# Moving the making of an attention-bias table from behind the first stage of a transformer layer into the middle of it

## The chip, the cores and the metric

One core of a Trainium2 chip. The kernel is one program on that core: TensorE (PE), VectorE (DVE), ScalarE (ACT), GpSimd (POOL), the DMA queue of SyncE (SP), and 16 DMA engines. The metric is device time in microseconds (us); lower is better. Times inside the kernel are microseconds from the start of the profiled span.

## The reference

One layer with sliding-window attention, then a gated embedding, over 512 tokens of width 2048 in float32. Cut to what matters:

```python
hn = rmsnorm(x, norm_g)
q, k, v, gate = split(hn @ w_in)            # 32 query heads, 4 key/value heads, 64 wide
scores = einsum(q, k) * 64**-0.5 + bias     # blocks of 128 queries, 256 keys
bias   = rel_bias[t5_bucket(distance)]      # 32 buckets x 32 heads
scores = where(0 <= distance < 128, scores, -inf)
out = softmax(scores, with one sink per head) @ v
x = x + (out * silu(gate)) @ w_out
x = x + (p @ ple_proj) * sigmoid(rmsnorm(x, ple_norm) @ ple_gate)
return rmsnorm(x, final_g)
```

The bias depends only on the distance between query and key, so per head it is a vector of 128 values. The kernel keeps one vector of 384 floats per head, filled with -3e38 where the distance is outside the window. This is the **table**. It is written to DRAM once and read back from there with an overlapping access pattern, so that each row of a bias tile is a shifted piece of it.

## The kernel before

Every product is made in three matmuls of a high and a low part (`fp32r`): a high part is a cast on ACT, a low part a subtraction on DVE. Weights arrive as raw tiles by DMA and are split in this way before PE can use them.

**First stage.** A loop over `k = 0..15` (the 16 row blocks of the weights) loads a block of the transposed input (`xr`, line 190) and a block of weights (`w`, line 195) on the SP queue, splits both, and adds up two blocks of queries (`qps`), the keys (`ktps`) and the values (`vps`) in PSUM. In the turns 3 to 6 it also loads the four token blocks `xn0` to `xn3` (line 236) and squares them on ACT (line 237). In turn 9 the inverse root mean square `rstd1` is made; POOL writes it to DRAM (`rdram`, line 241) and reads it back spread over all partitions (`rb`, line 242). `rb` scales the queries (line 257) and keys (line 280) as they leave PSUM.

**The table**, lines 318 to 331, follows the stage in the program: POOL loads `rel` (line 320), fills the vector with the mask (line 321), waits for the load, makes 17 small copies (lines 324 and 329) and writes the table `tdram` to DRAM (line 331). It works in the tile `misc`, a quarter of the pool `whole`, which has four buffers. `xn0` to `xn3`, `values`, `misc`, `diffs` and the gate tiles take turns in them.

**The stretch after it.** PE goes on with the remaining query blocks. `Weights` holds the raw tiles `wraw` (loaded on line 101), the high parts `whi` (line 107, ACT) and the low parts `wlo` (line 113, DVE), three buffers each. One raw tile serves eight k-steps of three matmuls. PE runs four times eight and then six more k-steps before the first attention scores.

**Weight sums.** Later products use sums of weight blocks, made in DRAM: SP copies a block (line 672) and POOL adds another with an accumulating DMA (line 674). `sum_weights(n)` issues the n-th of these steps. The calls stand in this order:

```python
    for n in range(SUM_FIRST):        # 8: four copies on SP, the first add on POOL
        sum_weights(n)
    load_bias(0)                      # SP, line 378: reads tdram into bias0
    ...                               # then W.split() with the loads of wraw, and more sums
```

The order of PE and of SP is the order in which the program is written, in the whole kernel. From the first sums on, this holds for all engines (`during`). In the first stage and up to the table, ACT, DVE and POOL are put in order by a planner, which works with estimated times; instructions of both kinds can mix. In the program as laid out, the planner has POOL do `rdram`, `rb`, four adds of line 674, and only then lines 320 to 331.

`load_bias(0)` on line 378 waits for the table in DRAM. It has a second wait: the pool `attn` takes the storage that the pool `start` of the first stage gave back, and `bias0` lies in the bytes of `w0s15`, the split weights of turn 15. So it also waits for the last `vps` matmul of that turn (line 228) and its last subtraction (line 208). SP is one queue in order: what stands behind line 378 waits with it, first of all the next three loads of `wraw`.

Of the kernel before, what the change touches and what calls it, by code (L numbers as in the profile page):

```python
# [11 lines left out]
F32 = mybir.dt.float32  # L12
# [8 lines left out]
P = 128  # L21
KC = D // P
NB = S // P
HEADS = 32
# [9 lines left out]
BUCKETS = 32  # L34
MAX_DIST = 128
WINDOW = 128
PLE = 256
EPS = 1e-6
MASKED = -3.0e38
TOEP = 384  # L40
# [4 lines left out]
def bucket_of(dist):  # L45
    exact = BUCKETS // 2
    d = np.maximum(dist, 1).astype(np.float32)
    large = exact + (
        np.log(d / exact) / np.log(MAX_DIST / exact) * (BUCKETS - exact)
    ).astype(np.int32)  # L50
    large = np.minimum(large, BUCKETS - 1)
    return np.where(dist < exact, dist, large).astype(np.int32)
# [3 lines left out]
def trunk_kernel(ctx: ExitStack, tc: tile.TileContext, a: dict):  # L56
    nc = tc.nc
# [22 lines left out]
    def quarter(name):  # L80
        return whole.tile([P, 4, S], F32, tag="quarter", name=name)
# [39 lines left out]
    def mm3(ps, sh, sl, mh, ml, first, last, more=False):  # L121


        nc.tensor.matmul(ps, sh, mh, start=first, stop=False, skip_group_check=more)  # L124
        nc.tensor.matmul(ps, sh, ml, start=False, stop=False, skip_group_check=more)  # L125
        nc.tensor.matmul(ps, sl, mh, start=False, stop=last, skip_group_check=more)  # L126
# [28 lines left out]
    def run(gen):  # L155
        for _ in gen:
            pass

    def rsqrt_mean(out, ssq, n, nm):

        w = out.shape[-1]
        ms = const.tile([P, w], F32, name=f"ms_{nm}")
        rt = const.tile([P, w], F32, name=f"rt_{nm}")
        y = const.tile([P, w], F32, name=f"y_{nm}")
        t = const.tile([P, w], F32, name=f"t_{nm}")
        nc.vector.tensor_scalar(ms, ssq, 1.0 / n, EPS, op0=ALU.mult, op1=ALU.add)
        nc.scalar.activation(rt, ms, AF.Sqrt)
        yield
        nc.vector.reciprocal(y, rt)
        nc.vector.tensor_mul(t, y, y)  # L170
        nc.vector.tensor_mul(t, t, ms)
        nc.vector.tensor_scalar(t, t, -0.5, 1.5, op0=ALU.mult, op1=ALU.add)
        nc.vector.tensor_mul(out, y, t)

    kinds, upto = [], {"q": 2, "g": 0}
    for kind in "qq" + "qqqqggg" * (KVH - 1) + "ggggggg":
        kinds.append((kind, upto[kind]))
# [6 lines left out]
    for k in range(KC):  # L186
        both = start_pool.tile([P, 2, 768], F32R, tag="w0s", name=f"w0s{k}")
        wh, wl = both[:, 0], both[:, 1]
        xg = start_pool.tile([P, S + 1], F32, tag="xr", name=f"xr{k}")
        nc.sync.dma_start(xg, a["xT"][k * P : (k + 1) * P, :])  # L190
        xr, g1 = xg[:, :S], xg[:, S:]
        w0 = w0s[0] if k == 0 else start_pool.tile([P, 768], F32, tag="w0", name=f"w0_{k}")
        cuts = [slice(512, 768), slice(0, 512)] if k == 0 else [slice(0, 768)]
        for c in cuts[-1:]:
            nc.sync.dma_start(w0[:, c], a["w_first"][k][:, c])
        room = acts if k < KC // 2 else more
        h = room.tile([P, S], F32R, tag="ah", name=f"xh{k}")
        l = room.tile([P, S], F32R, tag="al", name=f"xl{k}")
        nc.scalar.mul(h, xr, g1)
        if k == 0:  # L200
            nc.vector.tensor_copy(wh[:, cuts[0]], w0[:, cuts[0]])
            nc.vector.tensor_sub(wl[:, cuts[0]], w0[:, cuts[0]], wh[:, cuts[0]].bitcast(F32))
        nc.vector.scalar_tensor_tensor(
            out=l, in0=xr, scalar=g1, in1=h.bitcast(F32), op0=ALU.mult, op1=ALU.subtract
        )
        for c in cuts[-1:]:
            nc.scalar.copy(wh[:, c], w0[:, c])
            nc.vector.tensor_sub(wl[:, c], w0[:, c], wh[:, c].bitcast(F32))
        xh.append(h)
        xl.append(l)  # L210
        f, e = k == 0, k == KC - 1
        qc = [slice(512 + t * P, 512 + (t + 1) * P) for t in range(2)]
        if f:
            for n, (sw, mx) in enumerate(((wh, h), (wl, h), (wh, l))):
                for t in range(2):
                    nc.tensor.matmul(q_ps[t], sw[:, qc[t]], mx, start=n == 0, stop=False)
        else:
            for t in range(2):
                mm3(q_ps[t], wh[:, qc[t]], wl[:, qc[t]], h, l, f, e)
        for t in range(2):  # L220
            c = slice(t * P, (t + 1) * P)
            mm3(kt_ps[t], wh[:, c], wl[:, c], h, l, f, e)
        for t in range(NB):
            c = slice(t * P, (t + 1) * P)

            for part in "hl" if f else "lh":
                if part == "h":
                    nc.tensor.matmul(v_ps[t], h[:, c], both[:, :, 256:512], start=f, stop=e, skip_group_check=True)  # L228
                else:
                    nc.tensor.matmul(  # L230
                        v_ps[t][:, :256], l[:, c], wh[:, 256:512], start=False, stop=False, skip_group_check=True
                    )
        if 3 <= k < 3 + NB:
            t = k - 3
            xn = quarter(f"xn{t}").rearrange("p k t -> p (k t)")
            nc.sync.dma_start(xn, a["x"][t * P : (t + 1) * P, :])
            nc.scalar.activation(xn, xn, AF.Square, accum_out=ssq1[:, t : t + 1])
        if k == 9:
            run(rsqrt_mean(rstd1, ssq1, D, "r1"))
            rdram = tc.dram_tile([NB, P], F32, name="rdram")  # L240
            nc.gpsimd.dma_start(rdram.rearrange("t p -> p t"), rstd1)
            nc.gpsimd.dma_start(rb, rdram.rearrange("t p -> (t p)").partition_broadcast(P))
        if k == 10:
            for h in range(GROUP):
                nc.sync.dma_start(sinkb[QB * h : QB * h + QB], a["sinks"][h].partition_broadcast(QB))
            nc.sync.dma_start(pn, a["ple_norm"])
# [67 lines left out]
        )  # L314
    split(V[0], values[0])


    misc = quarter("misc")
    relb, tvec = misc[:HEADS, 1, :BUCKETS], misc[:HEADS, 2, :TOEP]
    nc.gpsimd.dma_start(relb, a["rel"])  # L320
    nc.gpsimd.memset(tvec, MASKED)
    exact = BUCKETS // 2
    bk = bucket_of(np.arange(WINDOW))
    nc.gpsimd.tensor_copy(tvec[:, P - 1 : P - 1 + exact], relb[:, :exact])
    for b in range(exact, BUCKETS):
        d = np.nonzero(bk == b)[0]
        if len(d):
            lo, n = P - 1 + int(d.min()), len(d)
            nc.gpsimd.tensor_copy(tvec[:, lo : lo + n], relb[:, b : b + 1].to_broadcast([HEADS, n]))
    tdram = tc.dram_tile([HEADS, TOEP], F32, name="tdram")  # L330
    nc.gpsimd.dma_start(tdram, tvec)

    pre.close()
    banks_s.close()
# [1210 lines left out]
    n = done[3]  # L1545
# [87 lines left out]
```

## Time and profile before

| | |
|---|---|
| median of 3 runs | 792.78 us (791.22 to 794.69) |
| the profiled execution | 791.03 us |
| its span | 789.3 us |
| PE busy | 778.5 us (99%) |
| DVE, ACT, POOL busy | 623.7, 506.5, 180.4 us |
| granted TensorE clock, mean | 0.997 |

The span is the time between the first and the last instruction of the profiled execution; 1.7 us of its time lie around it. Busy PE means that a matmul was in progress. The page cuts the span in 40 slices: PE shows 9 tenths or more in all but the last. The DMA engines show 6 tenths or more in all but the last two slices.

### The profile page before, as it was taken

What the parts mean: (1) busy time and instruction counts of PE and PEld (TensorE: products, weight loads), DVE (VectorE), ACT (ScalarE), POOL (GpSimd) and SP (SyncE); (2) the same over time, 40 slices, a digit from 0 to 9 for tenths busy, and PEclk for the clock granted to TensorE, in tenths of its full rate; (3) what the DMA queues carried; (4) which work ended last, traced back from release to release, by engine and by line L of the source; (5) the groups of instructions that cost most, each with busy time, mean ns of one, the idle gap of its engine ahead of it and who ended that gap; (6) DMA issues with size and microseconds to landing.
All of it is one profiled execution on the core that took longest, in us unless ns stands there. A gap on an engine that the chain in (4) does not pass through costs nothing.

```text
span 789.3 us, 11284 instructions
## 1 busy us (share of the span) xinstructions
PE 778.5 (99%) x3726; PEld 650.0 (82%) x3726; DVE 623.7 (79%) x1056; ACT 506.5 (64%) x1024; POOL 180.4 (23%) x394
## 2 busy tenths in 40 slices
PE   9999999999999999999999999999999999999995
PEld 8888788888888888888888888888888888888885
DVE  4446468887977788787886798999798988999686
ACT  5632366667666666565665655767788857967465
POOL 0002423544344414444143300200000021101000
PEclk9999999999999999999999999999999999999998
DMA  8797799999999999989997497998778999967833
GB/s 332 282 251 189 259 280 331 297 290 300 305 312 245 309 268 275 278 212 246 294 245 208 136 352 288 245 367 281 249 272 248 365 238 251 255 227 215 256 117 118
DMA packets 50634, 206.99 MB, mean 262 GB/s; under 512 B 7264, under 2 KB 8416, under 8 KB 44208
## 3 DMA queue, kind: packets, MB, share of 16 engines
q1 hardware_dynamic: 40240, 156.15, 54.7%
q0 software_dynamic: 9904, 49.61, 32.8%
q8 instruction: 29, 0.48, 0.2%
q10 hardware_dynamic: 432, 0.52, 0.2%
q14 instruction: 29, 0.24, 0.1%
HBM read 199.38 MB, written 78.69 MB: 352 GB/s over the span
## 4 chain that ended last, share of the span: by engine, by line
PE 92%; DMA 3%; DVE 2%; ACT 1%; issue 1%; SPq 0%; POOL 0%; ACTq 0%; DVEq 0%; POOLq 0%
PE gps L124 7%; PE gps L125 7%; PE gps L126 7%; PE qps L124 6%; PE qps L125 5%; PE qps L126 5%; PE g L125 5%; PE o L124 5%; PE g L124 5%; PE g L126 5%; PE o L125 5%; PE o L126 5%; DMA wraw<-in_w_q 2%; PE vps L228 2%; PE s L400 2%; PE o L522 2%
## 5 line engine op out<-in xcount | busy, mean ns | idle before, releaser
L124 PE MATMUL gps<-xh,whi 128*128 128x512 f32 x256 | 100.5, 393 | 0.0
L125 PE MATMUL gps<-xl,whi 128*128 128x512 f32 x256 | 100.1, 391 | 0.0
L126 PE MATMUL gps<-xh,wlo 128*128 128x512 f32 x256 | 99.9, 390 | 0.0
L113 DVE TENSOR_TENSOR wlo<-wraw,whi 128x1024 fp32r<-128x1024 f32 x60 | 74.6, 1246 | 30.5 <-ACT whi L107 17.2
L502 POOL TENSOR_SCALAR_AFFINE_SELECT own<-r 64x256 fp32r<-64x256 f32 x96 | 60.1, 626 | 162.2 <-DVE r L491 82.7
L126 PE MATMUL qps<-xh,wlo 128*128 128x512 f32 x224 | 87.5, 391 | 0.5 <-DVE wlo L113 0.5
L124 PE MATMUL qps<-xh,whi 128*128 128x512 f32 x224 | 87.7, 391 | 0.0
L125 PE MATMUL qps<-xl,whi 128*128 128x512 f32 x224 | 87.5, 391 | 0.0
L460 ACT ACTIVATE t<-t,sm 128x129 f32<-128x129 f32 x128 | 50.7, 397 | 51.7 <-DVE sm L451 48.8
L107 ACT CAST whi<-wraw 128x1024 fp32r<-128x1024 f32 x60 | 62.2, 1038 | 20.9 <-DMA wraw<-in_w_q 20.9
L710 DVE TENSOR_TENSOR blo<-braw,bhi 128x1024 fp32r<-128x1024 f32 x43 | 52.7, 1229 | 14.9 <-ACT bhi L709 14.9
L709 ACT CAST bhi<-braw 128x1024 fp32r<-128x1024 f32 x43 | 45.0, 1050 | 28.9 <-DMA braw<-in_ple_gate 9.5
L710 DVE TENSOR_TENSOR blo<-ring,bhi 128x1024 fp32r<-128x1024 f32 x48 | 58.3, 1223 | 4.7 <-ACT bhi L709 4.3
L709 ACT CAST bhi<-ring 128x1024 fp32r<-128x1024 f32 x48 | 50.2, 1049 | 17.9 <-PE o L126 14.1
L124 PE MATMUL g<-bhi,fhg 128*128 128x512 f32 x148 | 58.0, 392 | 0.0
L125 PE MATMUL g<-blo,fhg 128*128 128x512 f32 x148 | 57.8, 391 | 0.0
L126 PE MATMUL g<-bhi,flg 128*128 128x512 f32 x148 | 57.7, 390 | 0.0
L126 PEld LDWEIGHTS gps<-xh,wlo 128*128 128x128 f32 x256 | 48.1, 188 | 10.5
L124 PEld LDWEIGHTS gps<-xh,whi 128*128 128x128 f32 x256 | 48.1, 188 | 9.1
L483 ACT CAST r<-pt 128x256 fp32r<-128x256 f32 x64 | 23.8, 371 | 49.5 <-PE pt L478 49.3
L125 PEld LDWEIGHTS gps<-xl,whi 128*128 128x128 f32 x256 | 48.1, 188 | 8.6
L126 PEld LDWEIGHTS qps<-xh,wlo 128*128 128x128 f32 x224 | 42.1, 188 | 10.0 <-DVE wlo L113 1.0
(303 smaller groups left out, 2034.4 us busy)
## 6 DMA issues: line engine op xcount, KB each, us to landing
w_out<-in_w_out POOLq DMA_DIRECT2D x32, 512.0 KB, 9.2
wraw<-in_w_gate_in SPq DMA_DIRECT2D x32, 512.0 KB, 7.7
ring<-w_out SPq DMA_DIRECT2D x32, 512.0 KB, 4.7
wraw<-in_w_q SPq DMA_DIRECT2D x28, 512.0 KB, 9.3
braw<-in_ple_gate SPq DMA_DIRECT2D x22, 512.0 KB, 5.2
ring<-in_w_out SPq DMA_DIRECT2D x18, 512.0 KB, 5.5
ple_gate<-in_ple_gate SPq DMA_DIRECT2D x16, 512.0 KB, 10.0
ple_gate<-in_ple_gate POOLq DMA_DIRECT2D x16, 512.0 KB, 7.9
```

The costliest lines, as they stand in the source:

```text
L107: nc.scalar.copy(hi, self.raw[i])
L113: nc.vector.tensor_sub(lo, raw, hi.bitcast(F32))
L124: nc.tensor.matmul(ps, sh, mh, start=first, stop=False, skip_group_check=more)
L125: nc.tensor.matmul(ps, sh, ml, start=False, stop=False, skip_group_check=more)
L126: nc.tensor.matmul(ps, sl, mh, start=False, stop=last, skip_group_check=more)
L228: nc.tensor.matmul(v_ps[t], h[:, c], both[:, :, 256:512], start=f, stop=e, skip_group_check=True)
L400: nc.tensor.matmul(s_ps[:, u, : 2 * n], st, key[:, :, first : first + n], start=True, stop=True)
L460: nc.scalar.activation(su, su, AF.Exp, bias=sm[:, u : u + 1], accum_out=sm[:, 2 + u : 3 + u])
L483: nc.scalar.copy(r[:, 0], PT[i])
L502: nc.gpsimd.affine_select(out=cols(own[places[g % 2 ^ low]]), in_=cols(r[here, low].bitcast(F32)), pattern=[[sign * QB, 2], [0, GROUP], [s ...
L709: nc.scalar.copy(hi, raw)
L710: nc.vector.tensor_sub(lo, raw, hi.bitcast(F32))
```

## The change

The lines 318 to 331 become a function `bias_table()`, which is called in turn 8 of the first stage, ahead of turn 9 with `rdram` and `rb`. The instructions are the same. `misc` is now asked for ahead of `values`, right after `xn3`. `load_bias(0)` stays where it is, and the order on PE and SP is the same.

```diff
+    def bias_table():
+
+        misc = quarter("misc")
+        relb, tvec = misc[:HEADS, 1, :BUCKETS], misc[:HEADS, 2, :TOEP]
+        nc.gpsimd.dma_start(relb, a["rel"])
+        nc.gpsimd.memset(tvec, MASKED)
+        exact = BUCKETS // 2
+        bk = bucket_of(np.arange(WINDOW))
+        nc.gpsimd.tensor_copy(tvec[:, P - 1 : P - 1 + exact], relb[:, :exact])
+        for b in range(exact, BUCKETS):
+            d = np.nonzero(bk == b)[0]
+            if len(d):
+                lo, n = P - 1 + int(d.min()), len(d)
+                nc.gpsimd.tensor_copy(tvec[:, lo : lo + n], relb[:, b : b + 1].to_broadcast([HEADS, n]))
+        tdram = tc.dram_tile([HEADS, TOEP], F32, name="tdram")
+        nc.gpsimd.dma_start(tdram, tvec)
+        return tdram
...
+        if k == 8:
+            tdram = bias_table()
         if k == 9:
             run(rsqrt_mean(rstd1, ssq1, D, "r1"))
             rdram = tc.dram_tile([NB, P], F32, name="rdram")
...
     split(V[0], values[0])
 
-
-    misc = quarter("misc")
-    relb, tvec = misc[:HEADS, 1, :BUCKETS], misc[:HEADS, 2, :TOEP]
-    nc.gpsimd.dma_start(relb, a["rel"])
...
-    tdram = tc.dram_tile([HEADS, TOEP], F32, name="tdram")
-    nc.gpsimd.dma_start(tdram, tvec)
```

More of the change, by code (lines that the diff above doesn't have):

```diff
@@ L315, in trunk_kernel @@
     split(V[0], values[0])
-    misc = quarter("misc")
-    relb, tvec = misc[:HEADS, 1, :BUCKETS], misc[:HEADS, 2, :TOEP]
[L320 to L329, printed above, removed]
-    tdram = tc.dram_tile([HEADS, TOEP], F32, name="tdram")
-    nc.gpsimd.dma_start(tdram, tvec)
     pre.close()
```

## The prediction, made before the changed kernel ran

> **What bounds the kernel now.** I read the page first, then what PE waited for, then the SP and POOL queues around the moved lines, then the timelines of ACT, DVE and PE where these end.
>
> The page, parts 1 and 4:
>
> ```profile
> span 789.3 us, 11284 instructions
> PE 778.5 (99%) x3726; PEld 650.0 (82%) x3726; DVE 623.7 (79%) x1056; ACT 506.5 (64%) x1024; POOL 180.4 (23%) x394
> ```
>
> PE is idle for 789.3 - 778.5 = 10.8 us in the whole span. Nothing that leaves the matmuls alone can bring more than that. Most of it is out of reach, as the waits of PE show (us in total, times, longest):
>
> ```profile
> PE warm_ps L145 <- PEq L1623: 0.8, 1, 0.8
> PE qps L126 <- DVE wlo L113: 0.5, 1, 0.5
> PE o L524 <- POOL own L502: 0.3, 1, 0.3
> PE qps L216 <- ACT xh L199: 0.2, 1, 0.2
> ```
>
> Two of these are the start. The rest of the 10.8 us lies in the last slice (the stretch from 750 us):
>
> ```profile
> 750.00:789.30 39.30, 30.33 (x164) 26.21 (x162) 29.91 (x66) 23.60 (x43) 0.00 (x0) 0.93 0.35 117
> ```
>
> Here PE is busy 30.33 of 39.30, so 9.0 us are the end of the work, behind the last matmul. What is left for an edit near the first stage is 0.5 + 0.3 us. That is the first result: the change can hide a lot of waiting on SP and still gain less than 1 us.
>
> What it goes after is seen on SP:
>
> ```profile
> SPq L378 <- DMA tdram<-misc: 27.2, 1, 27.2
> SPq L378 <- PE qps L126: 0.6, 1, 0.6
> ...
> 82.36 0.72 SPq L378 DMA_DIRECT2D bias<-tdram  x1
> 83.15 0.87 SPq L101 DMA_DIRECT2D wraw<-in_w_q  x2
> ```
>
> SP stands at line 378 for 27.2 us, from 55 to 82.4, for the table, and the wait for PE, long fulfilled, comes behind it. Two loads of `wraw` stand behind it. Their way to PE:
>
> ```profile
> 87.01 1.05 ACT L107 CAST whi<-wraw 128x1024 fp32r<-128x1024 f32 x1 [13.07 <-DMA wraw<-in_w_q]
> 88.09 1.23 DVE L113 TENSOR_TENSOR wlo<-wraw,whi 128x1024 fp32r<-128x1024 f32 x1 [11.91 <-PE qps L125]
> 89.37 0.51 PE L126 MATMUL qps<-xh,wlo 128*128 128x512 f32 x1 [0.53 <-DVE wlo L113]
> ```
>
> So the late table costs PE 0.53 us at 89.37. ACT was idle for 13.07 us and DVE for 11.91 us ahead of it, but PE had three split tiles in hand and used them up.
>
> And this is why the table is late (POOL, start and duration):
>
> ```profile
> 37.68 0.95 POOL L241 DMA_DIRECT2D rdram<-rstd  x1 [36.30 <-DVE rstd L173]
> 50.94 0.58 POOL L242 DMA_DIRECT2D rb<-rdram  x1 [12.31 <-DMA rdram<-rstd]
> ...
> 65.78 0.80 POOL L320 DMA_DIRECT2D misc<-in_rel  x1
> 66.31 0.71 POOL L321 MEMSET misc<- 32x384 f32 x1
> 77.89 0.19 POOL L324 COPY misc<-misc 32x16 f32<-32x16 f32 x1 [10.87 <-DMA misc<-in_rel]
> 78.02 2.08 POOL L329 COPY misc<-misc 32x3 f32<-32x3 f32 x16
> 80.39 0.54 POOL L331 DMA_DIRECT2D tdram<-misc  x1 [0.30 <-POOL misc L329]
> ```
>
> with the DMAs from issue to landing (KB, us):
>
> ```profile
> rb<-rdram POOLq DMA_DIRECT2D x1, 256.0 KB, 6.4
> ...
> tdram<-misc POOLq DMA_DIRECT2D x1, 48.0 KB, 1.8
> ...
> rdram<-rstd POOLq DMA_DIRECT2D x1, 2.0 KB, 13.0
> misc<-in_rel POOLq DMA_DIRECT2D x1, 4.0 KB, 12.0
> ```
>
> **The moved part.** The work itself is the same: two DMAs, a memset, 17 copies. Ahead of 37.68 POOL had been idle for 36.30 us, so POOL pays nothing. `misc` now follows `xn3`, so it takes the first buffer to come free, that of `xn0`, whose square ends here:
>
> ```profile
> 13.71 1.92 ACT L237 ACTIVATE xn<-xn 128x2048 f32<-128x2048 f32 x1 [1.69 <-DMA xn<-in_x]
> 15.53 0.18 ACT L237 ACTIVATION_READ_ACCUMULATOR xn<-xn 128x1 f32 x1
> ```
>
> That is 13.71 + 1.92 = 15.6, or 15.7 with the read of the sum. I let the load of `rel` start at 16. Its landing is bounded by the same kind of row: 1.8 us (the table's own write) to 13.0 us (`rdram`, the longest of the four); I take 12.0, that of the same load. It lands at 18 to 29, likeliest 28. The copies take 0.19 + 2.08 = 2.3 us, to 30.4; the write is issued by 31 and lands between 33 and 44 by the same two bounds. SP asks for it at 55. So the wait of 27.2 us is gone, with 11 us to spare in the worst of these.
>
> **What is late next on SP.** The other waits of line 378. The last matmul on `w0s15`:
>
> ```profile
> 71.58 0.40 PE L228 MATMUL vps<-w0s,xh 128*128 128x512 f32 x1
> 71.81 0.40 PE L124 MATMUL qps<-xh,whi 128*128 128x512 f32 x1
> ```
>
> It ends at 71.98, and SP goes on at about 72.1 instead of 82.36. SP gains 10.3 us, not 27. The loads of `wraw` then go out at 83.15 - 10.3 = 72.9. In the trace the first was needed by ACT 87.01 - 83.15 = 3.9 us later; with twice that as the other end it lands at 77 to 81. The cast must also wait for a free `whi` buffer, which PE gives back after one tile, 24 matmuls. From 71.81 to the wait at 89.37 - 0.53 = 88.84 PE does three tiles and two matmuls more, 74 in all, 0.23 us each; 24 take 5.5 us, so the buffer is free at 77.3. The low part is then ready 1.05 + 1.23 us after 77.3 to 81, at 79.6 to 83.3. PE needs it at 88.84. At least 5.5 us to spare: the 0.53 us is gone in full.
>
> Of the 0.26 us at 132 I count half. It hangs on another chain:
>
> ```profile
> 132.03 0.39 PE L524 MATMUL o<-own,DV 128*128 128x256 f32 x1 [0.26 <-POOL own L502]
> ...
> 102.38 2.44 SPq L363 DMA_DIRECT2D DV<-diffs  x4
> ```
>
> SP has caught up before that point: line 363 at 102.38 waits for DVE in the attention loop, not for earlier loads. So from 102 on SP runs as before, and only the DMA backlog of 85 to 102 is smaller, which may or may not move POOL by a quarter of a microsecond. Ends 0 and 0.26, middle 0.13.
>
> **Costs of the new place.** The added DMA bytes are 52 KB beside
>
> ```profile
> 16.00:24.00 8.00, 8.00 (x40) 6.70 (x40) 3.36 (x4) 5.53 (x7) 0.00 (x0) 1.00 1.03 417
> ```
>
> 417 GB/s, so 0.12 us of full DMA engines. The loads of the stage have cover for it, since SP itself waits for free buffers there:
>
> ```profile
> SPq L190 <- DVE xl L203: 12.2, 8, 2.7
> SPq L195 <- DVE w0s L208: 11.7, 8, 3.1
> ```
>
> Without that cover it would cost those 0.12 us. On POOL the table is now ahead of `rdram`. POOL is free of it at 31 at the latest that I count, `rdram` is due at 37.68, so nothing is added. If it were, the slack is:
>
> ```profile
> 68.56 1.44 DVE L257 TENSOR_TENSOR rawq<-qps,rb 128x256 f32<-128x256 f32 x4 [4.91 <-PE qps L126]
> ```
>
> `rb` lands at 50.94 + 6.4 = 57.3; its first reader starts at 68.56 and waited for PE. PE asks for the first freed bank at 71.81, two of those four reads (0.72 us) later than 71.1. So `rb` may come 13.7 us later, and `rdram` be issued as late as 51.4, before PE stops. POOL's new wait is the one for the load of `rel`, up to 29. Behind it stand `rdram`, `rb` and four adds, and DVE waits for `rb`; that is the slack just named. After the four adds POOL finds the next add instead of the table, and SP issues the copy for it 10.3 us sooner. `values` now takes the buffer of `xn1`, free long before 71.
>
> **The sum.** 0.53 + 0.13 = 0.66 us off 791.03 us of the profiled execution: 790.4. The median of the runs is 1.75 us above that execution, so the median to expect is 792.78 - 0.66 = **792.1 us**. A measurement of this kernel tells about 0.5%, 4 us, from no change; this gain is a sixth of that.
>
> **The rivals.**
>
> *More gain than the profile shows.* The profiled execution, 791.03 us, is the quickest of the four times that I have. PE paid 0.53 us because the chain of `rel`, table, `bias0` and `wraw` was just that much too late, and each further microsecond of a DMA in it costs PE one. If the other executions are slower for this reason, the median falls to 790.4, the sum for the profiled one. For it: the DMAs of POOL vary between 1.8 and 13.0 us. Against: nothing in one trace shows the others. Chance 0.12. Even this is inside 0.5%, but for a tail of 0.03.
>
> *The planner leaves the table where it was.* POOL's order in this stage is the planner's, which put the table behind four adds before. If it still does so, the time stays at 792.8. Against: that order came with `misc` having to follow `values`, which is made at 71; now it follows `xn3`. Chance 0.08.
>
> *Slower: `rb` comes late.* POOL is held in the table past 51.4, and PE stops at 71.81 for the excess. For this the load of `rel` would have to land at 48.5, 32 us after its issue and 2.5 times the longest row; or the copies be stretched. Suppose `misc` gets the last of the four buffers (that of `xn3`, free at 29.1: its square is the last of the four) and lands at 42.1, and each of the 17 copies finds DVE in an instruction of up to
>
> ```profile
> 26.24 0.96 DVE L208 TENSOR_TENSOR w0s<-w,w0s 128x768 fp32r<-128x768 f32 x1
> ...
> 28.90 0.18 ACT L237 ACTIVATION_READ_ACCUMULATOR xn<-xn 128x1 f32 x1
> ```
>
> 0.96 us: 17 x 0.96 = 16.3 us more, free at 42.1 + 2.3 + 16.3 + 0.5 = 61.2, and PE stops for 61.2 - 51.4 = 9.8 us. That gives 792.8 + 9.8 = 802.6 at the far end, 797 to 798 halfway. In the trace of before the copies ran while DVE was idle (its row at 88.09 shows 11.91 us), so this price isn't seen there. The Trainium skill, "SBUF — State Buffer", section "Who interferes with whom", says that a DVE instruction with two SBUF inputs and a GpSimd instruction that reads SBUF shut each other out for a whole instruction; lines 203 and 208 are of that kind. By that rule the copies would be stretched at the new place, though only with both mishaps of place and landing would it reach PE; no run here shows it yet. Against the rival: with `xn0`'s buffer the table ends at 30.4 + 16.3 = 46.7 even then, still ahead of 51.4. Chance 0.12.
>
> **How the numbers follow.** Forecast (a stall gone, nothing else) 0.68, more gain 0.12, nothing moved 0.08, slower 0.12. The three runs of before lie 1.6 us below and 1.9 us above their median, so the forecast's own range is 790.4 to 794.5. Its lower end also holds the rival with more gain. I set the range at 789.8 to 795.2, which leaves out most of the slower rival and a little at either end. Faster by over 0.5% (under 788.8): the tail of 0.03 and 0.02 of scatter, 0.05. Slower by over 0.5% (over 796.7): 0.10 of the rival's 0.12, and 0.02 of scatter, 0.12. Within: 0.83.
>
> **What would show it.** Right: POOL's load of `rel` at 16, its copies before 32, `rdram` still at 37.7; SP at line 378 near 72 with a wait for PE in place of the table; the next `wraw` near 73; no wait of PE on line 113; PE idle for about 10.1 us. Wrong: `rdram` after 51 and DVE's first read of `rb` after 71; the four adds still ahead of the table; or a wait of PE over 1 us anywhere past 72.

## The result, and the profile after

| | median | its runs | profiled execution | its span |
|---|---|---|---|---|
| before | 793.94 us | 791.22 to 795.03 (6 runs) | 791.03 us | 789.3 us |
| after | 789.09 us | 788.95 to 790.41 (6 runs) | 789.11 us | 787.4 us |

The ratio is 0.9945, 95% interval 0.9926 to 0.9964: faster by 4.85 us in the medians. Between the two profiled executions it is 1.92 us. The forecast was a gain of 0.66 us, to 792.1 us, in a range of 789.8 to 795.2; the median of before is 1.2 us higher here than in the three runs that it started from. The median of after lies just under that range. The direction and the way were right, and the size was not.

PE and the chain on the page after:

```profile
span 787.4 us, 11284 instructions
PE 777.4 (99%) x3726; PEld 649.3 (82%) x3726; DVE 621.9 (79%) x1056; ACT 506.3 (64%) x1024; POOL 182.6 (23%) x394
...
PE 98%; DMA 0%; ACT 0%; DVE 0%; issue 0%; ACTq 0%; DVEq 0%
```

and what PE waited for after (us in total, times, longest):

```profile
PE warm_ps L145 <- PEq L1628: 0.8, 1, 0.8
PE qps L234 <- ACT xh L217: 0.2, 1, 0.2
```

Two waits are left, both at the start. The chain that ended last is 98% PE. The same line of the page before had a part of DMA in it:

```profile
PE 92%; DMA 3%; DVE 2%; ACT 1%; issue 1%; SPq 0%; POOL 0%; ACTq 0%; DVEq 0%; POOLq 0%
```

POOL after (start, duration, in brackets the idle time before):

```profile
16.20 0.70 POOL L181 DMA_DIRECT2D misc<-in_rel  x1 [14.83 <-ACT xn L255]
...
21.84 0.19 POOL L185 COPY misc<-misc 32x16 f32<-32x16 f32 x1 [4.48 <-DMA misc<-in_rel]
21.97 2.84 POOL L190 COPY misc<-misc 32x3 f32<-32x3 f32 x16
25.11 0.53 POOL L192 DMA_DIRECT2D tdram<-misc  x1 [0.31 <-POOL misc L190]
37.37 0.79 POOL L261 DMA_DIRECT2D rdram<-rstd  x1 [11.73 <-DVE rstd L173]
```

The write of the table is issued at 25.11, and `rdram` follows at 37.37, where it stood at 37.68 before. SP after, its waits at `load_bias(0)` (now line 383):

```profile
SPq L383 <- DVE w0s L226: 9.5, 1, 9.5
...
SPq L383 <- PE vps L246: 7.0, 1, 7.0
```

the timeline with its issues, and the first cast and subtraction that came late before:

```profile
71.72 0.72 SPq L383 DMA_DIRECT2D bias<-tdram  x1
72.50 0.87 SPq L101 DMA_DIRECT2D wraw<-in_w_q  x2
...
81.52 1.05 ACT L107 CAST whi<-wraw 128x1024 fp32r<-128x1024 f32 x1 [7.87 <-DMA wraw<-in_w_q]
...
82.60 1.22 DVE L113 TENSOR_TENSOR wlo<-wraw,whi 128x1024 fp32r<-128x1024 f32 x1 [6.71 <-PE qps L126]
```

SP still stands there, but for the storage of `w0s15` and only to 71.72. The low part starts at 82.60, PE needs it near 88: the stall is gone.

### The profile page after: what moved, and what is told of

Its sections match the earlier page's. It is cut to its first block, busy times and chain, and to the rows that moved or that the text cites. A ratio compares the mean times of both kernels' runs of the same rounds, so it can differ in the third digit from the quotient of the medians.

```text
span 787.4 us, 11284 instructions
## 1 busy us (share of the span) xinstructions
PE 777.4 (99%) x3726; PEld 649.3 (82%) x3726; DVE 621.9 (79%) x1056; ACT 506.3 (64%) x1024; POOL 182.6 (23%) x394
## 4 chain that ended last, share of the span: by engine, by line
PE 98%; DMA 0%; ACT 0%; DVE 0%; issue 0%; ACTq 0%; DVEq 0%
PE gps L124 7%; PE gps L125 7%; PE gps L126 7%; PE qps L124 7%; PE qps L126 7%; PE qps L125 7%; PE g L125 5%; PE g L124 5%; PE o L126 5%; PE o L125 5%; PE g L126 5%; PE o L124 5%; PE s L405 2%; PE o L527 2%; PE vps L246 2%; PE pt L483 2%
## 5 line engine op out<-in xcount | busy, mean ns | idle before, releaser
L113 DVE TENSOR_TENSOR wlo<-wraw,whi 128x1024 fp32r<-128x1024 f32 x60 | 73.5, 1226 | 25.3 <-ACT whi L107 17.3
```

The lines of the kernel that those rows point to most:

```text
L113: nc.vector.tensor_sub(lo, raw, hi.bitcast(F32))
```

## The experiments

**The question** was where the other 4 us come from. Three accounts were weighed. (1) SP standing at `load_bias(0)` costs, by more than the one stall that the profile of before showed. (2) POOL, held by the table, costs: its next add, the differences of the values and the first selects come late. (3) Part of it is memory traffic or chance, and would be seen in `before` at any place. Each text on record names its own theories; theory 1 is account (1) in all of them, and theory 2 one of the other two. Medians are compared among kernels that ran on the same chip beside the same runs of before.

All runs. "SP" is when SP passes `load_bias(0)`. The DMA share and the idle time of PE are from the table by windows of each profile (PE idle is the window less PE's busy time), in us:

| kernel | median (runs) | ratio to before, 95% | SP | DMA share 72-85 / 85-100 | PE idle 85-100 / 120-145 |
|---|---|---|---|---|---|
| before (profile of the prediction) | | | 82.36 | 0.27 / 1.00 | 0.53 / 0.26 |
| again | 793.52 (12) | 1.0003, 0.9982 to 1.0023 | 83.06 | 0.30 / 1.01 | 1.13 / 1.06 |
| again2 | 792.75 (1) | | 82.71 | 0.28 / 1.01 | 1.17 / 0.51 |
| after | 789.09 (6) | 0.9945, 0.9926 to 0.9964 | 71.72 | 0.88 / 1.01 | 0 / 0 |
| times2 | 795.91 (12) | 1.0031, 1.0013 to 1.0049 | 84.55 | 0.29 / 0.91 | 2.53 / 0 |
| times3 | 798.14 (9) | 1.0060, 1.0038 to 1.0083 | 87.37 | 0.29 / 0.75 | 5.29 / 0 |
| unblock | 793.36 (12) | 1.0010, 0.9991 to 1.0030 | 91.13 | 0.96 / 0.49 | 0 / 0.39 |
| unblock4 | 791.43 (12) | 0.9964, 0.9944 to 0.9983 | 92.12 | 1.01 / 0.78 | 0 / 0 |
| after_rb | 789.63 (6) | 0.9939, 0.9919 to 0.9960 | 71.74 | 1.00 / 1.03 | 0 / 0 |
| both | 789.74 (6) | 0.9938, 0.9919 to 0.9958 | 71.61 | 1.02 / 1.02 | 0 / 0 |
| hole | 798.64 (6) | 1.0052, 1.0033 to 1.0072 | 77.74 | 0.96 / 0.91 | 0 / 0 |
| pool_busy | 790.21 (12) | 0.9953, 0.9933 to 0.9972 | 72.31 | 0.95 / 0.98 | 0 / 0 |
| pool_late | 793.64 (12) | 0.9999, 0.9975 to 1.0023 | 82.41 | 0.38 / 1.02 | 1.09 / 1.33 |
| after_times3 | 789.55 (10) | 0.9948, 0.9928 to 0.9968 | 71.31 | 0.82 / 1.01 | 0 / 0 |

The kernel before had a median of 793.11 (32 runs, 790.94 to 799.59) beside again to unblock, 794.25 (17 runs) beside unblock4 to hole, and 793.53 (29 runs, 790.40 to 798.36) beside the last three and again2; `after` has the runs of the first table beside it.

**again, again2: the kernel before once more.** No edit.

> The kernel before, unchanged. Late weights (theory 1): PE's one wait for the low part near 88 us is what differs from one execution to the next. Times from 791 to 795 us, and in the profile the gap of PE near 88 is longer than the 0.92 us of the first profile by about what the execution is longer than 791.0 us; SP passes line 378 later than 82.4 by the same amount. Rival (theory 2, traffic): the executions differ in the stalls of 130 to 140 us, where PE waits for POOL, and line 378 passes within 0.5 us of 82.4.

> The kernel before once more, for another profile of it. Theory 1: line 378 is passed at 82 to 85 us; PE shows a gap at 88 to 92 and, as its time is nearer to 794 than to 791, gaps in 120 to 145 too. Rival (those later gaps are chance and have nothing to do with the table): no such gap at all, or gaps at other places.

The profiled execution of `again` took 793.33 us. PE around the first stall (start, duration, idle before):

```profile
87.90 0.39 PE L126 MATMUL qps<-xh,wlo 128*128 128x512 f32 x1
88.89 0.50 PE L124 MATMUL qps<-xh,whi 128*128 128x512 f32 x1 [0.60 <-ACT whi L107]
89.22 0.40 PE L125 MATMUL qps<-xl,whi 128*128 128x512 f32 x1
90.15 0.50 PE L126 MATMUL qps<-xh,wlo 128*128 128x512 f32 x1 [0.53 <-DVE wlo L113]
```

Two stalls stand where the profile of before has one. SP passed line 378 0.7 us later, at 83.06, so the high part was late too. Both the first gap and the gaps past 120 are larger than in the profile of before, and again2 shows them at the same places. With all 3726 matmuls of the two traces laid side by side from the first one on, `again` falls behind `after` by 0.3 us at the start, 1.7 at 86 to 92, 1.8 at 120 to 134, and 0.4 near 700: 4.2 us (times of `after`). again2 falls behind by 3.6 us in the same places, and the quick execution before by 1.9 us: 0.3 at the start, 0.91 at 88 to 90 and 0.82 at 130 to 138. At the two places that have to do with the table, the execution that the prediction rested on lost 1.7 us where `again` lost 3.5 and again2 3.0. The loss near 700, in `again` and again2 alone, was not followed up.

Why the gaps past 120 differ is seen in one cast, the one that starts near 118. From the timelines of ACT, in before:

```profile
117.07 1.05 ACT L107 CAST whi<-wraw 128x1024 fp32r<-128x1024 f32 x1 [1.59 <-DMA wraw<-in_w_q]
```

in again2:

```profile
118.56 1.05 ACT L107 CAST whi<-wraw 128x1024 fp32r<-128x1024 f32 x1 [2.35 <-DMA wraw<-in_w_q]
```

in again:

```profile
119.11 1.05 ACT L107 CAST whi<-wraw 128x1024 fp32r<-128x1024 f32 x1 [2.89 <-DMA wraw<-in_w_q]
```

and in pool_late, below, which has the same wait by other means:

```profile
119.41 1.05 ACT L107 CAST whi<-wraw 128x1024 fp32r<-128x1024 f32 x1 [3.39 <-DMA wraw<-in_w_q]
```

The later it starts, the more PE is idle in 120 to 145: 0.26, 0.51, 1.06, 1.33 us. In `after` it starts at 114.13 and waits for nothing. Four executions in one order are not yet a cause; the way from the cast to PE is followed in pool_late below.

**times2, times3: a later table.** The mask and the copies are made two or three times at the old place:

```diff
-    nc.gpsimd.memset(tvec, MASKED)
...
+    for _ in range(2):          # 3 in times3
+        nc.gpsimd.memset(tvec, MASKED)
+        ... # the 17 copies
```

> The kernel before, with the fill and the 17 copies of the table made twice, so that the table is later by one memset and 17 copies, about 3 us of POOL. Theory 1: line 378 passes 3 us later, PE's gap near 88 grows by 3 us, and the time by 2.5 to 3.5 us. Theory 2: POOL's own delay is passed on only where PE waits for POOL, so under 1 us.

> The same, made three times, about 6 us later. Theory 1: time up by 5 to 7 us against before, one gap of PE near 88 of about 7 us. Theory 2: under 2 us. If the loss is less than 1 for 1, something behind the gap gives time back.

SP passes 1.5 and 4.3 us later than in `again` (3 and 6 were expected), and PE's longest wait near 90 grows from 0.6 to 2.0 and 5.2 us: nearly one for one. The medians rise by 2.4 and 4.6 us over `again`. In times3:

```profile
93.56 0.79 PE L124 MATMUL qps<-xh,whi 128*128 128x512 f32 x1 [5.25 <-ACT whi L107]
...
95.41 0.63 PE L124 MATMUL qps<-xh,whi 128*128 128x512 f32 x1
95.84 0.63 PE L125 MATMUL qps<-xl,whi 128*128 128x512 f32 x1
```

After the stall the matmuls follow each other at 0.43 us instead of 0.23 until 99.7, and the granted clock in 85 to 100 is 0.77. So a long stall is paid for again in the clock; against `after` PE lost 8.8 us here, for 5.2 us of that wait. In exchange the gaps past 120 are gone, and no cast of line 107 between 100 and 145 waits for its load: the long stall lets the loads catch up.

**unblock, unblock4: the same late table, the SP step moved.** `load_bias(0)` is called after the second or the fourth group of eight k-steps:

```diff
-    load_bias(0)
...
+        if n == 1:          # 3 in unblock4
+            load_bias(0)
```

> The kernel before with the table where it was, but load_bias(0) called after the second group of eight k-steps, so that three loads of weights and two copies go ahead of it on SP. Theory 1 (only what stands behind line 378 on SP counts): no wait of PE for low parts near 88, and the time falls as with the moved table, to about 789 us (-3 to -5 against the median of before). Theory 2 (the table on POOL holds up the adds and the attention's POOL work): less than half of the gain, 791 or more, with the stalls near 132 and 137 still there.

> The kernel before with the table late on POOL, but load_bias(0) called only after the fourth group of eight k-steps, so that SP has little left to wait for when it gets there. Theory 1 (hole): no hole, so about 789 to 790 us. Theory 2 (POOL): as in the kernel before with load_bias after the second group, 792 to 794.

unblock gained nothing, 793.36 us. It is a miss for the plain form of account (1), and the profile tells why: other steps of POOL moved ahead of the table, which was written at 89.16 only, and SP stood 25.3 us at the later place. The hole in the DMA work moved with it (0.49 in 85 to 100), the gap at 88 went, and new ones came at 141 and 176. In unblock4 SP stood 6.0 us, and no gap is left at 88 or 120 to 145. The median went down by 2.8 us, 60% of the 4.6 us of after_rb beside it, with the table written as late as 89.67. The rest, 1.8 us, was not followed up; against `after`, its profile loses 0.4 us in the first 6 us and 1.0 us between 695 and 738.

**after_rb, both: how early must it be?** The first makes the table behind `rb`, held there by a copy of one element; the second is the changed kernel with `load_bias(0)` moved as in unblock.

```diff
+        nc.gpsimd.tensor_copy(relb[:1, :1], rb[:1, :1])
         nc.gpsimd.dma_start(relb, a["rel"])
```

> The changed kernel with the table tied to rb by one tiny copy on POOL, so that it is made between rb and the four adds, some 40 us later than in the changed kernel: the table lands near 74 to 78 and SP passes line 383 there. Theory 1: a hole 2 to 6 us longer than in the changed kernel, no gap of PE near 88, and 789 to 791 us. Theory 2: the four adds start 10 us later, so the gain is smaller, 791 to 793.

> The changed kernel and load_bias(0) called after the second group of k-steps, so that SP waits neither for the table nor for the last matmul of the first stage: the remaining 17 us of SP's wait (55 to 72) go too. Theory 1: DMA work starts up to 17 us sooner; PE has no waits left in the changed kernel's profile, so the time stays within 1 us, 788 to 789. Theory 2: the same. If it is slower, loads that come early collide with what PE needs in the first stage.

SP in after_rb, a wait and an issue:

```profile
SPq L383 <- DMA tdram<-misc: 15.2, 1, 15.2
...
71.74 0.72 SPq L383 DMA_DIRECT2D bias<-tdram  x1
```

SP waits 15.2 us for the table and still passes at 71.74 (74 to 78 was expected), since the storage comes free only then. The whole gain is there, 789.63 us: turn 8 isn't needed, only a table before 72. POOL's four adds start at 67.21 here, where they started at 61.71 before, and that costs nothing that the median shows. Moving SP's step as well brings nothing more (`both`, 789.74).

**hole: SP held back in the changed kernel.** Nine DVE instructions and a copy into `bias0` ahead of its load keep SP waiting.

```diff
+    nc.vector.memset(spare3, 0.0)
+    for _ in range(8):
+        nc.vector.tensor_add(spare3, spare3, spare3)
...
+        if kv == 0:
+            nc.vector.tensor_copy(biases[0], spare3[:, : P + HB])
```

> The changed kernel with its early table, but nine additions on DVE (idle there) and a copy into bias0 put ahead of load_bias(0), so that SP stands at line 383's place until about 82 as in the kernel before. POOL is left alone. Theory 1, now wider (a hole in the DMA work: what SP doesn't issue between 72 and 82 is missing later, while the DMA engines are full from 85 on): the gain is gone, 792 to 794 us, with PE's gap near 88 and the ones of 120 to 140 back. Theory 2 (the late table on POOL itself holds up the adds and the attention): the gain stays, 789 to 790.

This one doesn't tell the accounts apart. DVE did the copy ahead of low parts that PE needed:

```profile
78.78 0.79 PE L126 MATMUL qps<-xh,wlo 128*128 128x512 f32 x1 [5.10 <-DVE wlo L113]
```

SP stood only to 77.74, without a hole, and PE's idle time lies in 72 to 85, outside the columns of the table. What it does show is again the clock: PE fell 8.3 us behind `after` there, for a wait of 5.10 us.

**pool_busy, pool_late: SP and POOL apart.** Both are the changed kernel, in which POOL makes the table once more at the old place: load of `rel`, mask, copies. pool_busy writes nothing, so SP is free. pool_late also writes it over the first table, so SP stands. The order on PE, DVE, ACT and SP is that of the changed kernel.

```diff
     split(V[0], values[0])
+    nc.gpsimd.tensor_copy(relb[:1, :1], values[0][:1, :1])
+    nc.gpsimd.dma_start(relb, a["rel"])
+    ... # mask and 17 copies
+    nc.gpsimd.dma_start(tdram, tvec)      # pool_late alone
```

> The changed kernel, and at the table's old place POOL does the work of the table once more (load of rel, mask, 17 copies) and writes nothing to DRAM. SP's load_bias(0) needs only the early table, so SP is free; POOL is as busy and as late there as in the kernel before, or later (the second load can start only when values[0] is there, near 75 us). Theory 1 (the standing SP and the hole in the DMA work that it leaves are what costs): SP passes load_bias(0) at 72, the DMA engines stay above 85% busy from 72 to 85, and the time stays within 1 us of the change, 789 to 790 us; no PE gap at 88, none at 120 to 140 over 0.5 us. Theory 2 (POOL itself was late: its next add, and after it the diffs and the first selects): the time goes back to that of the kernel before, 792.5 to 794 us, with SP free.

> The same kernel, and its second table is also written over the first one in DRAM, so load_bias(0) waits again. The only difference to the run before is that SP stands (from 72 to about 85 us or a little later, since the second load starts only at about 76). Theory 1: 793 to 796 us, a hole in the DMA work in 72 to 85 (share under 0.4), PE gaps at 88 to 92 and some in 120 to 145. Theory 2: within 1 us of the run before, both at 792.5 to 794.

The 3.4 us between 790.21 and 793.64 come with that one write. First pool_busy, then pool_late, by windows (us, busy time of PE, PEld, DVE, ACT, POOL with counts, clock, DMA share, GB/s):

```profile
72.00:85.00 13.00, 13.00 (x59) 10.76 (x58) 7.30 (x14) 2.73 (x4) 3.05 (x15) 1.00 0.95 287
85.00:100.00 15.00, 15.00 (x68) 12.45 (x68) 6.67 (x12) 5.55 (x9) 10.73 (x22) 1.00 0.98 275
...
120.00:145.00 25.00, 25.00 (x127) 21.02 (x126) 21.32 (x50) 17.41 (x48) 10.54 (x21) 1.00 1.02 307
```

```profile
72.00:85.00 13.00, 13.00 (x59) 10.77 (x58) 3.98 (x10) 0.41 (x1) 3.46 (x20) 1.00 0.38 83
85.00:100.00 15.00, 13.91 (x61) 10.90 (x61) 8.81 (x11) 7.23 (x8) 8.54 (x12) 1.00 1.02 341
...
120.00:145.00 25.00, 23.67 (x117) 19.31 (x116) 22.16 (x49) 17.86 (x52) 10.11 (x26) 1.00 1.01 303
```

POOL was held longer where nothing was lost. The last copies of the second table, in pool_busy and in pool_late:

```profile
82.81 3.11 POOL L346 COPY misc<-misc 32x3 f32<-32x3 f32 x16
```

```profile
78.06 2.08 POOL L346 COPY misc<-misc 32x3 f32<-32x3 f32 x16
...
80.44 0.52 POOL L347 DMA_DIRECT2D tdram<-misc  x1 [0.30 <-POOL misc L346]
91.06 0.84 POOL L691 DMA_DIRECT2D small<-in_w_out  x1 [10.10 <-DMA small<-in_w_out]
```

pool_busy's POOL is done at 85.9 and goes straight on; pool_late's is done at 81 and then idles for 10.10 us, for a block that SP has to copy first. Account (2) falls: POOL is late because SP is. What a busy POOL may still cost is within the 0.7 us between pool_busy and after_times3, which ran beside it; in its profile PE loses nothing to `after` between 10 and 690 us. Account (3) falls for these 3.4 us: they come and go with SP's wait.

Now the way from SP to the gaps past 120 can be followed in pool_late. From the chain of work, the pieces between 100 and 125 us (start, duration):

```profile
104.69 0.59 SPq L380
...
105.33 14.06 DMA wraw<-in_w_q
...
119.41 1.06 ACT whi L107
```

and the timelines of DVE and PE behind it:

```profile
120.49 1.22 DVE L113 TENSOR_TENSOR wlo<-wraw,whi 128x1024 fp32r<-128x1024 f32 x1 [3.94 <-ACT whi L107]
...
123.22 0.41 DVE L508 TENSOR_TENSOR r<-pt,r 128x256 fp32r<-128x256 f32 x1
...
123.68 0.39 PE L539 MATMUL o<-r,V 128*128 128x256 f32 x1 [0.96 <-DVE r L508]
```

A load of raw weights issued at 105.33 takes 14.06 us. ACT, an engine in order, waits for it at the cast; DVE waits for the cast; behind the subtraction on DVE stands the `r` of the softmax, and PE stops for `r`. PE has no wait for these weights themselves past 92. It is the attention step queued behind them that is late. The second gap, where PE waits for POOL's `own` (0.3 us in pool_late and `again`), was not followed in this way; in the quick execution before, where it is the only one, the profile's chain comes to it from the cast at 117.07, by the softmax on DVE and `own` on POOL.

**after_times3: does the new place cost anything?** The table filled and copied three times in turn 8 (the edit of times3, at the new place).

> The changed kernel with the table filled and copied three times in its new place. Both theories, and the sum of the prediction, hold the new place for free while the table lands before 72: two more fillings of about 4 us each push the table's write from 25 to about 33 us, ahead of rdram at 37. Expected the time of the change, 789 to 790 us. If the place has a cost of its own (a shared port between POOL and DVE), two more fillings show it: over 791.

789.55 us, the time of the change; POOL wrote the table at 35.00 and `rdram` at 36.97. The third round of copies took more than twice the 2.08 us of the old place:

```profile
29.44 5.25 POOL L191 COPY misc<-misc 32x3 f32<-32x3 f32 x16
```

So the place stretches the copies, and the time of the kernel doesn't show it: the new place is free as long as POOL is done ahead of `rdram`.

## Why the prediction was right or wrong

**Right: the moved part.** `rel` loaded at 16.20 (forecast 16), copies before 32, `rdram` at 37.37, SP at 71.72 (72.1) with the wait for `w0s15` in the table's place, the next `wraw` at 72.50 (72.9), no wait of PE on line 113, PE idle 787.4 - 777.4 = 10.0 us (10.1). The load of `rel` was sized too long (12 us taken, landed within 5.5), the first cast at 81.52 came 0.5 us behind the end of the range given for its landing; neither reached PE. The rivals of a planner that leaves the table where it was and of a late `rb` did not come about: DVE's first read of `rb` starts at 68.27.

**The stretched copies.** The 16 copies took 2.08 us in before, pool_late and after_rb, where DVE stood idle meanwhile; 2.84 in turn 8; 3.11 in pool_busy with DVE busy for 1.98 of them; and 3.39, 3.36 and 5.25 in after_times3, the last with DVE busy for 4.33 of 5.30 us. That is up to 3.2 us more for all of them, not the 16.3 us of the rival's far end. The rule of the Trainium skill, "SBUF — State Buffer", section "Who interferes with whom", bore out in direction.

**Wrong: the term 0.53 + 0.13 = 0.66 us.** Three steps of the working failed.

1. "The late table costs PE 0.53 us": idle time before a matmul was taken for the price of the stall. The matmul ahead of the gap in the profile of before:

```profile
88.45 0.40 PE L125 MATMUL qps<-xl,whi 128*128 128x512 f32 x1
```

The next starts at 89.37, 0.92 us later where 0.23 is the pace; a further 0.12 goes in the step from 89.37 to 89.72, and 0.07 in that from 88.15 to 88.45. The stall cost 0.69 + 0.12 + 0.07 = 0.88 us. A matmul is shown 0.39 us long while one starts each 0.23, so the modelled tail hides part of every gap. The bound "0.5 + 0.3 us" for an edit near the first stage failed with it: the same 3726 matmuls kept PE busy for 778.5 us before and 777.4 after, so 1.1 of the 1.9 us between the two profiles came out of busy time and 0.8 out of idle time.

2. "From 102 on SP runs as before, and only the DMA backlog of 85 to 102 is smaller": SP doesn't run as before. Two of its loads, first before, then after:

```profile
104.87 0.92 SPq L101 DMA_DIRECT2D wraw<-in_w_q  x1
...
115.72 0.33 SPq L101 DMA_DIRECT2D wraw<-in_w_q  x1
```

```profile
103.98 0.59 SPq L101 DMA_DIRECT2D wraw<-in_w_q  x1
...
107.97 0.59 SPq L101 DMA_DIRECT2D wraw<-in_w_q  x1
```

After the change they go out 0.9 and 7.8 us sooner. PE itself is 1.2 us ahead there, so the first says little; the second does. Between the two, SP waited 4.8 + 2.3 us for transfers of `DV` to land in before, and 0.2 us in after: the backlog held SP too. Nor is the backlog small: 13 us at a DMA share of 0.27 are not made up in a stretch where the DMA engines stand at 1.00. (On the page of before one slice besides the last two is under 6 tenths: that of 434 to 454 us shows 4.) Loads land late, and hold ACT and DVE in order. The load issued at 104.87 was cast 12.2 us later, when it had come; the one issued at 103.98 was cast after 10.2 us and not waited for. The forecast gave all this 0.13 us; matmul against matmul it cost 0.82 us at 130 to 138 in the quick execution and 1.8 in `again`.

3. "More gain than the profile shows", chance 0.12: this rival won, and it was priced too low as well. It named the right sign, that the profiled execution was the quickest of the four and that a chain just too late costs more when it is later; of the places past 120 it says nothing. Its price, 790.4, came from the gap to the median of three runs. Runs of before spread over 790.4 to 799.6, those of after over 788.95 to 790.41, and those of after_rb, both, pool_busy and after_times3 over 788.86 to 790.57: where SP passes by 72.4, most of the spread is gone with the stalls.

With 1 and 2 in their measured sizes (0.88 + 0.82, and 0.3 us of scatter at the start) the difference of the two profiled executions, 1.9 us, is whole to 0.1 us. Of the 4.2 us of `again`, an execution near the median, 3.5 lie in the same two places. The 4.85 us of the medians were not taken apart: no execution of before above 793.33 us was profiled, and what makes one execution land a load at 117 and another at 119 stays open.

## What to carry to other kernels

When an engine in order stands and its work is the issue of loads, count the bytes not moved and ask where the DMA engines next have room for them; if they are full from there on, as here, the price can fall due far behind the wait, at whatever is queued behind the late loads on the engines that consume them. Price a stall of PE from start to start, against the pace, not by the idle time before it. And where a wait ends within a microsecond of need, one profile, above all the quickest, isn't the kernel: take a second one before putting a number on it.

## What the runs showed of the hardware

A stall of PE costs clock behind it. If the clock is either whole or half, which the pace of 0.43 instead of 0.23 us nearly says, a mean of 0.89 over a window of 15 us stands for 2 x (1 - 0.89) x 15 = 3.3 us at half. By this estimate it was 3.3 us in times2 (waits of 2.0 and 0.5 us), 2 x (1 - 0.77) x 15 = 6.9 us in times3 (5.2 us) and 2 x (1 - 0.74) x 13 = 6.8 us in hole (5.1 us). Stalls of 0.5 to 1.0 us left the clock at 1.00 in every profile. The Trainium skill, "TensorE: Matmul & The Clock Gate", section "What's actually happening", puts the clock at half after an idle window of about 3.4 us, counted in free-running windows. The times at half pace agree with one and two such windows; that a wait of 2.0 us, followed by two matmuls and one of 0.5 us, was enough is sooner than the page's figure.

The load of the 4 KB of `rel` took 12.0 us at its old place in before and 5.5 in turn 8 and in after_rb. At the place of the second table the copies that wait for it began 8.3 us after its issue in pool_busy and 4.0 in pool_late. 512 KB of `wraw` were there 3.9 us after their issue (83.15 to 87.01 in before) when the DMA engines had been mostly idle (a share of 0.27 in 72 to 85), and took 14.06 us in the backlog.
